# Feed-forward of a trunk layer: sums made ahead take the buffers of gated tiles and GpSimd's queue, and a pass's first operands come in front of the residual

## The chip, the cores and the metric

The kernel runs on one core of a Trainium2 chip. Its time is the device time of one execution, in microseconds (us). The engines of a core work side by side, each through its own list of instructions in order: TensorE (PE; its weight loads are PEld) does matrix products into eight PSUM banks, VectorE (DVE), ScalarE (ACT) and GpSimd (POOL) do elementwise work, and SyncE (SP) does nothing here but issue DMAs. ScalarE and GpSimd issue DMAs too, in the same list as their other work (ACTq and POOLq). An instruction that waits holds up everything behind it on its engine.

## The reference

One layer (DEPTH = 1) on 2048 tokens of width 1024, all float32: a spatial-gating mixer and a cross attention into 256 memory tokens, projected and added to the input, a layer norm, then the part that matters here:

```python
def swiglu_ffn(x, w_in, w_down):
    h = x @ w_in
    return (jax.nn.silu(h[..., :D_FF]) * h[..., D_FF:]) @ w_down

x = layer_norm(DEEPNORM_ALPHA * x + swiglu_ffn(x, ffn_w_in[i], ffn_w_down[i]), ln2_g[i], ln2_b[i])
```

`w_in` is 1024 x 5632, `w_down` 2816 x 1024, so the hidden width is 22 tiles of 128 rows.

## The kernel before

**Exactness.** A float32 product is made of three fast ones. `split` (L71) writes the rounded value (ScalarE's cast, L73) and the remainder (VectorE's subtraction, L74), and `PASSES` multiplies high by high, high by low and low by high. Data lies feature-major, with tokens along the free dimension.

**Seven products.** Matrices are cut in 2 x 2 blocks and multiplied with seven block products in place of eight (a Strassen-Winograd scheme). That needs sums of blocks on both sides. `halves` (L120 on) loads two row tiles of weights (`r_u`, loads at L125) and makes four sums, s1 to s4 (L132, L133, L135, L136), on GpSimd for tiles f < 5 and on VectorE for f >= 5. `products` (L145 on) walks the seven in an order, splits each operand, and runs 12 matmuls on it; after each product a "stage" empties PSUM (L391 to L402).

**Passes and blocks.** The tokens go through the FFN in three passes of 688, 680 and 680. A pass goes through the 22 hidden tiles in blocks (5, 4, 4, 4, 5 tiles in pass 0; 4, 4, 4, 4, 6 in the others). For each tile `up` (L384) makes the two halves of the hidden layer and gates them; after a block `down` or `down7` adds the block's share to the output. In pass 0 `whole` (L418) puts a gated tile, split, into pool "g", and `down` (L558) makes ordinary products. In passes 1 and 2 all blocks but the last go through `down7` (L503), seven products for each pair of output row tiles, with `left` (L456) bringing the operands of one pair: five loads, of which two read `w_down` itself (L479) and three read sums that were made and split before (L90, L464, L471).

**Sums made ahead.** What pass 0 splits for the up products it also stores in DRAM (`keep`, L81, on ScalarE's queue, `k_u`), and passes 1 and 2 read it back (`ready`). For `down7` the sums are made during pass 0: at each of the tiles f = 5 to 20 `left_sums` (L482) makes those of one block and pair, sixteen in all. It is a generator that is moved on once at each of the seven stages of an up tile: load (L485, through `tiles4`), four sums on GpSimd (L491), then two steps that split and store. A leftover of an earlier layer norm (`norm_work`) is moved on in the same way.

**Buffers.** A tile belongs to a pool with so many buffers, and an instruction that writes a new tile waits until all users of the buffer's former tile are done, stores included. "raw" has 4 (`r_u` two a tile, `r_es` and `r_ses` of `left_sums`, `r_d` and `r_e` of the down stages), "wsp" 5 (every split operand; an up tile uses seven, `left_sums` two), "g" 7 (gated tiles; in passes 1 and 2 the seven operands `gp` of `down7`), "sums" 4, "acc" 4 (the residual and result `fa` of a pass, one for each pair of row tiles).

**Order.** TensorE's order is that of the program (`in_order`). The other lists are laid out when the kernel is built, by a planner that goes by what is ready in its own estimate of time and prefers what comes earlier in the program. So the sums of a next tile may stand between the stages of this one.

**The start of a pass.** In passes 1 and 2 the main loop (L998 on) makes the up tiles of block 0 and one of the next block, exhausts `norm_work`, and calls `residual` (L551: four loads from `x1d` into "acc", each of which needs the stores of the pass before, L590, to be done with that buffer). Then `down7` begins with its first `left`.

Of the kernel before, what the change touches and what calls it, by code (L numbers as in the profile page):

```python
# [17 lines left out]
P = 128  # L18
# [21 lines left out]
def trunk_kernel(ctx, tc, xT, memT, wv, wuq, ws, bs, vg, vb, wmk, wmv, wo,  # L40
# [27 lines left out]
    def raw(shape, name):  # L68
        return common.tile(shape, F32, tag="raw", bufs=4, name=name)

    def split(hi, lo, src, engine=nc.vector):  # L71

        nc.scalar.copy(hi, src)  # L73
        engine.tensor_sub(lo, src, hi.bitcast(F32))  # L74

    def wsp(shape, name):
        return common.tile(shape, F32R, tag="wsp", bufs=5, name=name)
# [267 lines left out]
    class Pass:  # L345
# [110 lines left out]
        def left(self, blk, m, f0, q):  # L456

            name, key = f"e{self.no}_{blk}_{m}", f"e{blk}_{m}"
            v = self.tiles4(m, f0, q, name)
            t = ready(f"{key}_5", f"56_{name}")  # L460
            out = {5: t[:, 0], 6: t[:, 1]}
            t = wsp([P, 2, 2, q, P], f"w17_{name}")
            out[1], out[7] = t[:, 0], t[:, 1]
            nc.sync.dma_start(out=t[:, 1].bitcast(F32), in_=kept[f"{key}_7"])  # L464
            split(t[:, 0, 0], t[:, 0, 1], v[:, 0, 0])
            t = wsp([P, 2, 2, q, P], f"w24_{name}")
            out[2], out[4] = t[:, 0], t[:, 1]
            for x in range(2):
                split(t[:, x, 0], t[:, x, 1], v[:, x, 1])
            r = raw([P, 2, q, P], f"w3_{name}")  # L470
            nc.sync.dma_start(out=r, in_=kept[f"{key}_3"])  # L471
            out[3] = r.bitcast(F32R)
            return out

        def tiles4(self, m, f0, q, name):

            r = raw([P, 2, 2 * q, P], f"r_{name}")
            for a in range(2):
                nc.sync.dma_start(out=r[:, a], in_=w2[m + a, :, f0:f0 + 2 * q, :])  # L479
            return r.rearrange("p a (i j) x -> p a j i x", j=2)  # L480

        def left_sums(self, blk, m, f0, q):  # L482

            name, key = f"es{blk}_{m}", f"e{blk}_{m}"
            v = self.tiles4(m, f0, q, name)  # L485
            s = raw([P, 4, q, P], f"r_s{name}")
            yield
            a11, a12, a21, a22 = (v[:, a, j] for a in range(2) for j in range(2))
            for n, (x, y, op) in enumerate(((a21, a22, ALU.add), (s[:, 0], a11, ALU.subtract),
                                            (a11, a21, ALU.subtract), (a12, s[:, 1], ALU.subtract))):  # L490
                nc.gpsimd.tensor_tensor(out=s[:, n], in0=x, in1=y, op=op)  # L491
                yield
            for n, pa in enumerate((5, 7)):
                t = wsp([P, 2, 2, q, P], f"w{pa}_{name}")
                split(t[:, :, 0], t[:, :, 1], s[:, 2 * n:2 * n + 2])
                if n == 0:
                    keep(f"{key}_5", t)
                else:
                    keep(f"{key}_7", t[:, 0])
                    keep(f"{key}_3", t[:, 1])  # L500
                yield

        def down7(self, blk, q, f0, last):  # L503

            h, n, gp = self.h, self.n, self.gp
            if blk == 0:
                self.u = [open_pools["sums"].tile([P, 4, P], F32, tag="sums", name=f"fu{self.no}_{m}")
                          .rearrange("p a b -> p (a b)")[:, 0:h] for m in range(0, KD, 2)]
            w = [self.left(blk, 0, f0, q)]
            banks = []  # L510

            def product(j, p):
                y, u = self.out[j], self.u[j]
                c11, c12, c21, c22 = (y[:, a, b * h:(b + 1) * h] for a in range(2) for b in range(2))
                n, start, stop = {1: (0, True, False), 6: (1, True, True), 2: (0, False, True), 5: (2, True, False),
                                  7: (3, True, False), 3: (2, False, True), 4: (3, False, True)}[p]
                bk = banks[j][n]
                for i in range(q):
                    for x, (a, b) in enumerate(PASSES):
                        matmul(bk, w[j][p][:, a, i, :], gp[p][:, i, b], start=start and i == 0 and x == 0,  # L520
                               stop=stop and i == q - 1 and x == 2, skip_group_check=True)
                if p == 6 and blk == 0:
                    nc.scalar.copy(u, bk)
                    return
                to = {1: u, 6: u, 2: c11, 5: c22, 7: c22, 3: c12, 4: c21}[p]
                if blk == 0 and p in (2, 5, 3, 4):
                    nc.vector.scalar_tensor_tensor(out=to, in0=to, scalar=ALPHA, in1=bk, op0=ALU.mult, op1=ALU.add)
                else:
                    nc.vector.tensor_add(to, to, bk)  # L529

            def second(j):
                for p in (2, 3, 4):
                    product(j, p)
                if last:
                    y, u = self.out[j], self.u[j]
                    nc.vector.tensor_add(y[:, 0, h:n], y[:, 0, h:n], u)
                    nc.vector.tensor_tensor(out=y[:, 1].rearrange("p (b t) -> p b t", b=2),
                                            in0=y[:, 1].rearrange("p (b t) -> p b t", b=2),
                                            in1=u.unsqueeze(1).broadcast_to([P, 2, h]), op=ALU.add)

            for j in range(KD // 2):
                if j < KD // 2 - 1:
                    w.append(self.left(blk, 2 * j + 2, f0, q))
                banks.append([bank(f"e{i}_{self.no}_{blk}_{j}")[:, 0:h] for i in range(4)])
                for p in (6, 1, 5, 7):
                    product(j, p)
                if j:
                    second(j - 1)
            second(KD // 2 - 1)
# [427 lines left out]
    for no in range(len(FPASSES)):  # L977
# [20 lines left out]
        for blk, nb in enumerate(blocks):  # L998
            end = blk == len(blocks) - 1
            fs = range(f0 + len(ahead), f0 + nb)  # L1000
            if no and not end:
                ys = list(ahead)
                for f in fs:
                    ys.append(up(f))
                    if len(ys) % 2 == 0:
                        side.append((pa.pair(len(ys) // 2 - 1, blk, ys[-2][1], ys[-1][1]), 2))
                ahead = [up(f0 + nb)]
            else:
                gs = [pa.whole(*y) for y in ahead] + [pa.whole(*up(f)) for f in fs]
                ahead = []  # L1010
            if blk == 0:
                for _ in norm_work:
                    pass
                pa.residual()
            if no and not end:
                pa.down7(blk, nb // 2, f0, blk == len(blocks) - 2)
            elif not end:
                pa.down(blk, gs, f0, whole, lambda ci, m: None)
            elif no < len(FPASSES) - 1:
# [92 lines left out]
```

## Time and profile before

| | |
|---|---|
| median of 3 runs | 2264.46 us (2261.26 to 2265.94) |
| the profiled execution | 2261.46 us, its span 2259.6 us |
| TensorE busy | 2118.9 us, 94% of the span |
| VectorE, ScalarE, GpSimd busy | 71%, 40%, 17% |
| mean granted TensorE clock | 0.979 of full speed |
| moved by DMA | 408 MB, 181 GB/s |
| up stages of pass 0, blocks 1 to 4 | 878.6 to 949.5, 979.6 to 1050.6, 1082.4 to 1153.0, 1184.7 to 1282.3 us |
| first `down7` of pass 1, of pass 2 | from 1396.0 us, from 1852.2 us |

How to read the profile: a line of groups gives the source line, engine, operation, "written <- read" with shapes, the count, the busy time, the mean of one in ns, and after the second bar the idle time of the engine just before them, with what ended it. Names come from the tiles: `h` are PSUM banks of an up tile, `d` of `down`, `e` of `down7`; `s_u`, `r_u`, `w` belong to the up products, `r_es`, `r_ses`, `w_es`, `k_e` to the sums made ahead, `w_e` to the operands that `left` brings. A line in order of time starts with its start and its duration and joins like neighbours. "SPq" is SyncE's DMA queue.

### The profile page before, as it was taken

Reading aid. Unit: us, or ns where it says so; the run is one execution under the profiler, and the core shown is the slowest. Engines: PE = TensorE matmul, PEld = TensorE weight load, DVE = VectorE, ACT = ScalarE, POOL = GpSimd, SP = SyncE. Lnnn points to the kernel's source line nnn. Section 1 sums busy time; section 2 is a strip of 40 time slices with the busy share of each in tenths; the row PEclk is TensorE's granted clock in tenths of the full one; section 3 lists DMA queues with packets and bytes.
Section 4 is the critical chain, followed back from the end, with each engine's and each line's share of the span. In section 5 each row is a group of like instructions: output and inputs, shape, how many; then the busy total and the mean of one; then the engine's idle time right before and its main releaser. Section 6 shows DMA issues by size and latency. Waiting matters only on the chain.

```text
span 2259.6 us, 35072 instructions
## 1 busy us (share of the span) xinstructions
PE 2118.9 (94%) x12938; PEld 1995.0 (88%) x12938; DVE 1614.5 (71%) x2966; ACT 908.3 (40%) x1814; POOL 389.7 (17%) x318
## 2 busy tenths in 40 slices
PE   9899999999999889898898898999999989999997
PEld 7888888798788789788888788999999979999996
DVE  7987896796798876666667676566666765666656
ACT  5553743653554443333324344223323342233234
POOL 1402322321331611111111140000000400000002
PEclk9999999999999999999999899999999999999998
DMA  6234233425235474645556557666665576666653
GB/s 206 75 115 138 93 109 116 133 67 162 97 98 164 171 249 171 231 182 205 207 193 224 178 198 259 224 239 217 233 231 176 174 260 237 227 226 231 227 181 99
DMA packets 152331, 408.12 MB, mean 181 GB/s; under 512 B 15456, under 2 KB 25696, under 8 KB 152160
## 3 DMA queue, kind: packets, MB, share of 16 engines
q1 hardware_dynamic: 132096, 341.89, 45.3%
q10 hardware_dynamic: 19584, 62.92, 7.2%
q8 instruction: 102, 1.67, 0.3%
q0 software_dynamic: 480, 1.07, 0.2%
q14 instruction: 69, 0.57, 0.1%
HBM read 326.13 MB, written 79.69 MB: 180 GB/s over the span
## 4 chain that ended last, share of the span: by engine, by line
PE 61%; DVE 18%; DMA 9%; issue 5%; ACT 4%; POOL 2%; ACTq 0%; SPq 0%; DVEq 0%; POOLq 0%
PE h L60 30%; PE e L60 9%; PE d L60 9%; PE v L60 5%; DMA r_u<-in_w 3%; PE u L60 3%; DVE w L74 2%; DMA r_x<-in_xT 2%; PE y L60 2%; DVE w_o L74 1%; DVE w_u L74 1%; DVE x L74 1%; POOL s_a L233 1%; ACT p L740 1%; DVE z L697 1%
## 5 line engine op out<-in xcount | busy, mean ns | idle before, releaser
L60 PE MATMUL h<-x,w 128*128 128x340 f32 (+1 forms) x5544 | 910.1, 325 | 67.4 <-DVE w L74 20.7
L60 PEld LDWEIGHTS h<-x,w 128*128 128x128 f32 x5544 | 886.1, 192 | 87.0 <-DVE w L74 29.4
L60 PE MATMUL d<-g,w_d 128*128 128x344 f32 (+3 forms) x1632 | 266.9, 324 | 12.2 <-ACT w_d L73 6.6
L60 PEld LDWEIGHTS d<-g,w_d 128*128 128x128 f32 x1632 | 260.5, 191 | 17.1 <-ACT w_d L73 7.4
L60 PE MATMUL e<-gp,w_e 128*128 128x340 f32 x1344 | 214.4, 321 | 14.7 <-DMA w_e<-k_e 14.7
L60 PEld LDWEIGHTS e<-gp,w_e 128*128 128x128 f32 x1344 | 212.6, 190 | 15.4 <-DMA w_e<-k_e 15.2
L60 PE MATMUL y<-br,w_o 128*128 128x512 f32 x960 | 224.2, 395 | 0.0
L60 PEld LDWEIGHTS y<-br,w_o 128*128 128x128 f32 x960 | 180.5, 188 | 41.8
L73 ACT CAST w<-r_u 128x512 fp32r<-128x512 f32 x198 | 122.0, 617 | 183.6 <-PE h L60 117.5
L60 PE MATMUL v<-w_v,x 128*128 128x512 f32 x768 | 188.2, 401 | 6.4 <-ACT w_v L73 4.8
L74 DVE TENSOR_TENSOR w<-r_u,w 128x512 fp32r<-128x512 f32 x198 | 150.0, 758 | 49.8 <-ACT w L73 42.3
L60 PEld LDWEIGHTS v<-w_v,x 128*128 128x128 f32 x768 | 143.6, 190 | 42.2 <-ACT w_v L73 4.8
L60 PE MATMUL u<-xt,w_u 128*128 128x256 f32 x768 | 95.6, 279 | 0.0
L369 POOL TENSOR_TENSOR t<-r_f,r_f 128x340 f32<-128x340 f32 (+1 forms) x12 | 13.9, 1156 | 461.9 <-DVE c L392 376.7
L60 PEld LDWEIGHTS u<-xt,w_u 128*128 128x128 f32 x768 | 92.7, 188 | 0.0
L529 DVE TENSOR_TENSOR fa<-fa,e 128x340 f32<-128x340 f32 x128 | 64.6, 506 | 38.1 <-PE e L60 36.0
L491 POOL TENSOR_TENSOR r_ses<-r_es 128x256 f32<-128x256 f32 x32 | 28.8, 920 | 362.7 <-DMA r_es<-in_w 181.5
L60 PE MATMUL u<-x,w_u 128*128 128x256 f32 x576 | 77.8, 286 | 11.9 <-DVE u L706 7.1
L73 ACT CAST w_d<-r_d 128x384 fp32r<-128x384 f32 (+2 forms) x104 | 52.7, 519 | 88.8 <-PE d L60 65.6
L74 DVE TENSOR_TENSOR w_o<-r_o,w_o 128x512 fp32r<-128x512 f32 (+1 forms) x96 | 69.0, 728 | 21.4 <-ACT w_o L73 21.3
L60 PEld LDWEIGHTS u<-x,w_u 128*128 128x128 f32 x576 | 71.4, 189 | 14.6 <-issue 7.0
L393 ACT ACTIVATE c<-c 128x340 f32<-128x340 f32 (+1 forms) x66 | 32.3, 489 | 128.6 <-DVE c L392 128.6
(206 smaller groups left out, 2894.5 us busy)
## 6 DMA issues: line engine op xcount, KB each, us to landing
w<-k_u SPq DMA_DIRECT2D x176, 512.0 KB, 4.3
r_u<-in_w SPq DMA_DIRECT2D x88, 512.0 KB, 3.6
k_u<-w ACTq DMA_DIRECT2D x88, 512.0 KB, 3.4
r_u<-in_wuq SPq DMA_DIRECT2D x32, 512.0 KB, 3.2
r_o<-in_wo SPq DMA_DIRECT2D x32, 512.0 KB, 3.5
r_e<-in_w SPq DMA_DIRECT2D x64, 256.0 KB, 2.9
w_e<-k_e SPq DMA_DIRECT2D x64, 256.0 KB, 3.2
w_e<-k_e SPq DMA_DIRECT2D x32, 512.0 KB, 4.0
```

Of the source, the lines that this page charges most:

```text
L60: in_order(nc.tensor.matmul(*args, **kw))
L73: nc.scalar.copy(hi, src)
L74: engine.tensor_sub(lo, src, hi.bitcast(F32))
L233: nc.gpsimd.tensor_add(self.s2, self.s2, sq)
L369: nc.gpsimd.tensor_sub(t3, b22, b12)
L393: nc.scalar.activation(c12, c12, AF.Silu)
L491: nc.gpsimd.tensor_tensor(out=s[:, n], in0=x, in1=y, op=op)
L529: nc.vector.tensor_add(to, to, bk)
L697: nc.vector.tensor_scalar(z[h][:, b], z[h][:, b], mv[:, b, 0:1], rs[:, b:b + 1], ALU.subtract, ALU.mult)
L740: nc.scalar.activation(pr[:, h, :], svs[h // 2][:, h % 2, :], AF.Exp, scale=HD ** -0.5, bias=mxv[:, h:h + 1], accum_out=sm[:, h:h + 1])
```

## The change

Two things are changed.

1. `left_sums` takes both its tiles, r and s, from pool "g" (they have a fixed shape of 4 x q x 128 a partition, 4 KB, under a gated tile's 5.5 KB). Its two loads are issued on GpSimd's queue (`tiles4` with a tile given). It no longer takes "wsp" tiles: when the four sums are done, the high halves are written over r and the low halves over s, in place. The stores stay on ScalarE's queue; there are four of 256 KB (high and low of each pair of sums) in place of one of 512 KB and two of 256 KB, into DRAM tiles that interleave high and low, so that what was the tile `_3` is now the second half of `_7`. `left` reads the same data as before, out of that half.
2. In passes 1 and 2 the first `left` of a block is called by the main loop and handed to `down7`. For block 0 that is ahead of `residual`; for the other blocks the order of the program is the same as before.

```diff
@@ -461,52 +461,51 @@
-            nc.sync.dma_start(out=t[:, 1].bitcast(F32), in_=kept[f"{key}_7"])
+            nc.sync.dma_start(out=t[:, 1].bitcast(F32), in_=kept[f"{key}_7"][:, 0])
...
             r = raw([P, 2, q, P], f"w3_{name}")
-            nc.sync.dma_start(out=r, in_=kept[f"{key}_3"])
+            nc.sync.dma_start(out=r, in_=kept[f"{key}_7"][:, 1])
             out[3] = r.bitcast(F32R)
             return out
 
-        def tiles4(self, m, f0, q, name):
-
-            r = raw([P, 2, 2 * q, P], f"r_{name}")
+        def tiles4(self, m, f0, q, name, r=None):
+
+            queue = nc.sync if r is None else nc.gpsimd
+            r = raw([P, 2, 2 * q, P], f"r_{name}") if r is None else r
             for a in range(2):
-                nc.sync.dma_start(out=r[:, a], in_=w2[m + a, :, f0:f0 + 2 * q, :])
+                queue.dma_start(out=r[:, a], in_=w2[m + a, :, f0:f0 + 2 * q, :])
             return r.rearrange("p a (i j) x -> p a j i x", j=2)
 
         def left_sums(self, blk, m, f0, q):
 
             name, key = f"es{blk}_{m}", f"e{blk}_{m}"
-            v = self.tiles4(m, f0, q, name)
-            s = raw([P, 4, q, P], f"r_s{name}")
+            r, s = (open_pools["g"].tile([P, 4, q, P], F32, tag="g", name=f"{x}_{name}") for x in "rs")
+            v = self.tiles4(m, f0, q, name, r.rearrange("p (a i) j x -> p a (i j) x", a=2))
             yield
             a11, a12, a21, a22 = (v[:, a, j] for a in range(2) for j in range(2))
             for n, (x, y, op) in enumerate(((a21, a22, ALU.add), (s[:, 0], a11, ALU.subtract),
                                             (a11, a21, ALU.subtract), (a12, s[:, 1], ALU.subtract))):
                 nc.gpsimd.tensor_tensor(out=s[:, n], in0=x, in1=y, op=op)
                 yield
+            hi, lo = r.bitcast(F32R), s.bitcast(F32R)
             for n, pa in enumerate((5, 7)):
-                t = wsp([P, 2, 2, q, P], f"w{pa}_{name}")
-                split(t[:, :, 0], t[:, :, 1], s[:, 2 * n:2 * n + 2])
-                if n == 0:
-                    keep(f"{key}_5", t)
-                else:
-                    keep(f"{key}_7", t[:, 0])
-                    keep(f"{key}_3", t[:, 1])
+                k = slice(2 * n, 2 * n + 2)
+                split(hi[:, k], lo[:, k], s[:, k])
+                t = kept[f"{key}_{pa}"] = dram.tile([P, 2, 2, q, P], F32, tag=f"{key}_{pa}", name=f"k_{key}_{pa}")
+                for x, part in enumerate((r, s)):
+                    nc.scalar.dma_start(out=t[:, :, x], in_=part[:, k])
                 yield
 
-        def down7(self, blk, q, f0, last):
+        def down7(self, blk, q, f0, last, w):
...
-            w = [self.left(blk, 0, f0, q)]
             banks = []
@@ -1008,12 +1007,15 @@
+            seven = no and not end
+            if seven:
+                first = [pa.left(blk, 0, f0, nb // 2)]
             if blk == 0:
                 for _ in norm_work:
                     pass
                 pa.residual()
-            if no and not end:
-                pa.down7(blk, nb // 2, f0, blk == len(blocks) - 2)
+            if seven:
+                pa.down7(blk, nb // 2, f0, blk == len(blocks) - 2, first)
```

## The prediction

> **What bounds the kernel now.** I began with the stretches of the span by engine, one row per stage. In pass 0 the up stages of blocks 1 to 4 (tiles f = 5 to 21, the ones with sums made ahead up to f = 20) are rows 1, 2, 3 and 4; the fifth row is a part of pass 1.
>
> ```profile
> core 0: us, PE busy (x) PEld busy (x) DVE busy (x) ACT busy (x) POOL busy (x), PEclk, DMA share, GB/s
> 878.60:949.50 70.90, 59.02 (x340) 55.75 (x338) 50.90 (x83) 28.14 (x55) 11.79 (x12) 0.95 0.67 237
> 979.60:1050.60 71.00, 58.66 (x339) 55.64 (x337) 48.38 (x81) 28.37 (x55) 11.75 (x12) 0.95 0.64 229
> 1082.40:1153.00 70.60, 58.57 (x338) 55.28 (x336) 49.10 (x81) 28.30 (x55) 11.82 (x12) 0.95 0.66 230
> 1184.70:1282.30 97.60, 79.48 (x434) 75.26 (x432) 62.29 (x106) 36.52 (x72) 12.71 (x13) 0.88 0.60 209
> 1430.00:1666.00 236.00, 236.00 (x1515) 236.00 (x1514) 153.15 (x312) 69.12 (x151) 0.00 (x0) 1.00 0.66 228
> ```
>
> In pass 1 TensorE never stops. In pass 0 it does, and its granted clock falls to 0.95 and 0.88. The chain of waits says what 84 matmuls of an up tile should cost: in the first row 72 of them run without a gap, 11.38 / 72 × 84 = 13.3 us a tile. Seventeen tiles would be 226 us; the four stretches together are 70.9 + 71.0 + 70.6 + 97.6 = 310.1. So 84 us are lost here, the largest loss in the FFN.
>
> ```profile
> 979.63 11.38 PE h L60 x72
> 1399.95 5.88 DMA w_e<-k_e
> ```
>
> Next the instructions in order of time of one such stage (the second row): first TensorE's, then SyncE's DMA queue, then one line of VectorE and one of ScalarE. In brackets stands the idle time before, and what ended it.
>
> ```profile
> 979.47 22.85 PE L60 MATMUL h<-x,w 128*128 128x344 f32 x144
> 1005.40 5.58 PE L60 MATMUL h<-x,w 128*128 128x344 f32 x24 [3.08 <-DVE c L401]
> 1013.16 9.67 PE L60 MATMUL h<-x,w 128*128 128x344 f32 x50 [2.19 <-ACT w L73]
> 1024.74 1.84 PE L60 MATMUL h<-x,w 128*128 128x344 f32 x10 [1.90 <-DVE w L74]
> 1030.40 14.01 PE L60 MATMUL h<-x,w 128*128 128x344 f32 x84 [0.90 <-DVE w L74]
> 1045.90 1.84 PE L60 MATMUL h<-x,w 128*128 128x344 f32 x10 [1.50 <-DVE w L74]
> 1049.93 2.53 PE L60 MATMUL d<-g,w_d 128*128 128x344 f32 x7 [2.19 <-ACT w_d L73]
> ```
> ```profile
> 988.39 0.80 SPq L479 DMA_DIRECT2D r_es<-in_w  x2
> 995.70 1.30 SPq L125 DMA_DIRECT2D r_u<-in_w  x2
> 1018.16 0.84 SPq L125 DMA_DIRECT2D r_u<-in_w  x2
> ```
> ```profile
> 1004.14 0.69 DVE L132 TENSOR_TENSOR s_u<-r_u 128x512 f32<-128x512 f32 x1 [5.26 <-DMA r_u<-in_w]
> 1004.40 0.62 ACT L73 CAST w_es<-r_ses 128x512 fp32r<-128x512 f32 x1 [3.31 <-DMA k_u<-w]
> ```
>
> The story is in these lines. The pool "raw" has four buffers. An up tile needs two (r_u); the sums made ahead need two more (r_es and r_ses). So the next tile's r_u is issued alternately with r_es and only when those are given back: at 995.70, while the first of its sums stands in VectorE's order already. VectorE waits 5.26 us for the landing, and behind it stand the additions that empty PSUM (L401) and the low halves of the weights (L74): TensorE stops 3.08, then 2.19, then 1.90 us. ScalarE has a stop of its own there: the cast for the ahead sums waits 3.31 us for a "wsp" buffer that a store still reads. The totals, from the groups by line and from the queue's waits (the latter count the mixer too):
>
> ```profile
> L132 DVE TENSOR_TENSOR s_u<-r_u 128x512 f32<-128x512 f32 x17 | 11.7, 691 | 41.7 <-DMA r_u<-in_w 41.7
> L491 POOL TENSOR_TENSOR r_ses<-r_es 128x256 f32<-128x256 f32 x32 | 28.8, 920 | 362.7 <-DMA r_es<-in_w 181.5 <-DVE w_d L74 130.4 <-DVE w L74 35.9
> SPq L125 <- POOL r_ses L491: 54.1, 13, 5.1
> SPq L125 <- DMA r_es<-in_w: 37.1, 17, 3.3
> ```
>
> **Part 1: the ahead sums leave "raw" and "wsp".** Both r and s of L482 to L501 now come from pool "g", and the halves are written in place over them. "raw" then holds r_u of two tiles, and r_u of tile f+1 can be issued once tile f-1 has given its two buffers back, about a tile time (13 us) before it is wanted, against the 8.4 us from issue at 995.70 to use at 1004.14. So VectorE's 41.7 us of waits should go. What is late next? VectorE's own work. Rows 1 to 3 hold 48.4 to 50.9 us of it in four tiles, under the 53.2 us that TensorE needs for four, so it still fits, though at 91 to 96%, and some of it can move into the down stages in between, where it is idle for 13 of 32 us:
>
> ```profile
> 1050.60:1082.40 31.80, 31.75 (x192) 31.75 (x193) 18.54 (x32) 5.80 (x10) 2.85 (x4) 0.95 0.44 151
> ```
>
> I don't expect the whole 84 us. Three prices for a tile after the change: 13.3 us (all loss gone: 226 us for seventeen, a gain of 84); the 84 matmuls at 1030.40 with the gap before them, 14.01 + 0.90 = 14.9 us, a stretch where no load is late; and 16.4 us, from 1024.74 to 1047.74 (1045.90 + 1.84), where 118 matmuls take 23.0 us with VectorE still catching up. I take the middle one, since the catching up is caused by the late load: 17 × 14.9 = 253, and the 2.19 us ahead of the down stage, which the late load doesn't make, stays three times: 6.6. So 260 in place of 310: **50 us** less. With 16.4 it is 279 + 6.6, a gain of 25. The bounds of this part are 25 and 84, and there is a loss only by the rival below.
>
> Pool "g" must have room. It has seven buffers; at the k-th tile of a block k-1 hold gated tiles and two the sums before, which leaves 6-k, two at k = 4. Only the first tile of blocks 2 to 4 finds one free, and there 30 us of a down stage lie between. I cost it at nothing; without that cover it is one store's landing, 4.0 us, three times:
>
> ```profile
> k_e<-w_es ACTq DMA_DIRECT2D x16, 512.0 KB, 3.1
> k_e<-w_es ACTq DMA_DIRECT2D x32, 256.0 KB, 4.0
> r_es<-in_w SPq DMA_DIRECT2D x32, 256.0 KB, 3.0
> wm<-in_ws POOLq DMA_DIRECT2D x1, 512.0 KB, 6.5
> 5.03 0.53 POOL L603 DMA_DIRECT2D wm<-in_ws  x1
> 1013.96 2.21 POOL L491 TENSOR_TENSOR r_ses<-r_es 128x256 f32<-128x256 f32 x2 [18.28 <-DVE w L74]
> 1014.35 1.23 DVE L74 TENSOR_TENSOR w<-r_u,w 128x512 fp32r<-128x512 f32 x1
> ```
>
> **Part 2: the two loads move from SP's queue to GpSimd's.** Thirty-two issues leave SP, and GpSimd gets 32 × 0.53 us, 1.06 us a tile, on an engine that is busy 11.8 of 71 us. A load on that queue landed after 6.5 us (512 KB, at the start of the kernel) against 3.0 us on SP's. Behind the waiting issue on GpSimd stand only the four additions of L491 (0.92 us each and the like), and for those waits the cast in ScalarE's order. The loads are free of "raw" and can run a tile ahead, so I cost this at 0; uncovered it is 6.5 - 3.0 + 1.06 = 4.6 us a tile, 73 us for sixteen.
>
> The Trainium skill, SBUF — State Buffer, section "SBUF: two separate sides", speaks against this move: descriptors of a DMA issued from GpSimd are written by its cores, which are locked out while VectorE holds the shared ports, and it advises ScalarE's or SyncE's queue instead. The same page, section "A bandwidth-pool intuition that's wrong (but worth ruling out)", gives 620 ns alone and 3100 ns overlapped for one such DMA; as an estimate from that page, 2.5 us × 32 loads would be 79 us if nothing hid them. Contention of the two engines shows in this trace (the VectorE operation at 1014.35 took 1.23 us beside GpSimd's additions, the one at 1004.14 without them 0.69); a GpSimd-issued load beside VectorE's work, none here shows.
>
> **Part 3: the stores.** Four of 256 KB a tile on ScalarE's queue in place of one of 512 and two of 256: the same bytes, one issue more, in runs of half the length in DRAM. Nearest row: 4.0 us to landing. Nothing of the up products waits for these any more. ScalarE is busy 28 of 71 us, so 0; not below nothing, because no store goes; at most an issue of about 0.8 us on the path, 16 × 0.8 = 13. Reading `_7` and `_3` out of one DRAM tile keeps 256 KB a load: 0.
>
> **Part 4: a pass's first operands ahead of the residual.** SyncE's queue, TensorE and ScalarE at the start of the down stage of pass 1, block 0:
>
> ```profile
> 1393.10 0.37 SPq L554 DMA_DIRECT2D fa<-x1d  x1
> 1394.07 5.83 SPq L554 DMA_DIRECT2D fa<-x1d  x3
> 1399.95 0.63 SPq L464 DMA_DIRECT2D w_e<-k_e  x1
> 1401.17 0.36 SPq L464 DMA_DIRECT2D w_e<-k_e  x1
> ```
> ```profile
> 1389.09 0.39 ACT L73 CAST w_e<-r_e 128x256 fp32r<-128x256 f32 x1
> 1396.00 2.96 PE L60 MATMUL e<-gp,w_e 128*128 128x340 f32 x18
> 1405.88 19.37 PE L60 MATMUL e<-gp,w_e 128*128 128x340 f32 x114 [6.91 <-DMA w_e<-k_e]
> 1862.92 17.40 PE L60 MATMUL e<-gp,w_e 128*128 128x340 f32 x100 [7.78 <-DMA w_e<-k_e]
> ```
>
> Three products (18 matmuls) run, and the fourth waits 6.91 us for L464, which stood behind four residual loads. ScalarE's cast at 1389.09 writes the other half of the same tile, so its buffer was free before the first residual at 1393.10. Ahead of the residual the load is there in time. But the second group's L464 (1401.17) stays behind: its product 7 is wanted 42 matmuls after 1396.00, 42 × 2.96 / 18 = 6.9 us, at 1402.9, and its load, issued at about 1400 with the same 5.9 us, lands at 1406. So some 3.1 us stay, and 3.8 and 4.7 are won: I take 3 a pass, **6 us** in all, because the residual now lands a little later too and the addition L527 needs it. Bounds: 0, if the second group's wait takes all of it, and 14.7.
>
> **Sum.** 50 + 6 = 56 us off the profiled execution's own 2261.46 (span 2259.6), 2205.5; the median of the runs shown stands 3.0 us above that execution, so I predict **2208**.
>
> **Rivals.**
> 1. VectorE becomes the bound. For it: 91 to 96% of the time of the matmuls, and 1.23 us operations beside GpSimd. Against: the first tiles of each stage already run without a gap. Tiles at 16.4 us: gain 25, with part 4 about 31: 2233.
> 2. All the loss goes, the clock back to 1.00 as in pass 1: 84 + 14.7 = 99: 2166. Against: the fourth tile still has 1.50 and 2.19 us of gaps of other makers.
> 3. Slower: GpSimd's loads come late, at the cast of the ahead sums (L495). ScalarE takes its list in order, so behind that cast wait the high halves of the next weights and L393, and for them TensorE. Price 4.6 us a tile, 73 in all, less the 56 won: 17 more, 2281. It decides from 56 / 16 = 3.5 us of stop a tile. For it: 6.5 us against 3.0. Against: "g" has a free pair of buffers at nearly every tile, so that the load has a tile's time. The SBUF page of the Trainium skill, quoted in part 2, is for this rival.
> 4. It does nothing: r_u stays late, because r_d of the down stages takes the free "raw" buffers or the order of SP's queue doesn't move. Against: SP waited for r_es and r_ses by name. About 2262.
>
> **Chances.** Forecast (gain 40 to 70 us) 0.53; rival 1 0.22; rival 2 0.10; rival 3 0.08; rival 4 0.07. Forecast and rivals 1 and 2 are all faster by more than 0.2% (4.5 us, about what can be told from no change here): faster 0.85, same 0.07, slower 0.08. The range leaves out most of rivals 3 and 4 and the far end of 2: from 2264 - 86 = 2178 to 2250, above rival 1 by its unpriced stores of 13 us and some.
>
> **What would show it.** VectorE's group L132 without its 41.7 us of DMA waits; r_u issues of SP a tile ahead; the up stages of blocks 1 to 3 at 58 to 64 us and the last at 72 to 80, granted clock near 1.00; the wait on w_e of the fourth product gone and one of about 3 us three products later. Wrong: TensorE or ScalarE waiting for GpSimd's r_ses, up stages still near 71 us, or a wait of the first addition L527 for the residual.

## The result, and the profile after

The changed kernel takes 2200.40 us (median; 2199.23 to 2201.72), the kernel before on the same chip 2264.69 us: a ratio of 0.972, 95% interval 0.970 to 0.974. The prediction was 2208. The profiled execution of the changed kernel has a span of 2197.5 us against 2259.6, 62.1 us less.

Read first the stretches by engine (as in the prediction: the busy time of each engine in a stretch, then the granted clock). Rows 1 to 3 are the up stages of pass 0, blocks 1 to 3; row 4 is that of block 4 with 1.8 us of the down stage behind it; row 5 is the down stage of block 2.

```profile
core 0: us, PE busy (x) PEld busy (x) DVE busy (x) ACT busy (x) POOL busy (x), PEclk, DMA share, GB/s
876.60:934.20 57.60, 54.19 (x338) 52.73 (x336) 44.91 (x78) 25.37 (x50) 13.30 (x16) 1.00 0.73 259
965.50:1023.00 57.50, 54.09 (x337) 52.62 (x337) 43.53 (x75) 25.39 (x50) 10.43 (x13) 1.00 0.72 249
1054.30:1112.00 57.70, 54.29 (x337) 52.82 (x336) 43.72 (x76) 25.39 (x50) 10.34 (x13) 1.00 0.71 249
1143.40:1217.00 73.60, 69.42 (x432) 67.69 (x432) 57.02 (x101) 33.77 (x68) 9.27 (x11) 1.00 0.71 247
1023.00:1054.30 31.30, 30.54 (x194) 30.26 (x195) 23.23 (x39) 8.05 (x15) 9.66 (x12) 1.00 0.62 215
```

The stages of four tiles fell from about 71 to 57.6 us, and the granted clock in them is 1.00 where it was 0.95 and 0.88. VectorE has 43.5 to 44.9 us of work in them (before: 48.4 to 50.9), and the down stage between them took some of it over, 23.23 us where it had 18.54.

For comparisons I take a stage exactly, from its first matmul to the first of the next stage. The four up stages are then 305.8 us before (70.3 + 70.5 + 70.1 + 94.9; the prediction's stretches, 310.1, took in the starts of down stages) and 244.7 after (57.5 + 57.6 + 57.7 + 72.0): **61.0 us of the 62.1 lie there.**

TensorE's instructions in order of time, in the second of these stages and the first two of the down stage; in brackets the idle time before and what ended it:

```profile
965.31 40.26 PE L60 MATMUL h<-x,w 128*128 128x344 f32 x252
1006.00 0.58 PE L60 MATMUL h<-x,w 128*128 128x344 f32 x2 [0.43 <-ACT w L73]
1007.81 11.60 PE L60 MATMUL h<-x,w 128*128 128x344 f32 x72 [1.23 <-DVE w L74]
1020.31 1.85 PE L60 MATMUL h<-x,w 128*128 128x344 f32 x10 [0.90 <-DVE w L74]
1022.87 0.58 PE L60 MATMUL d<-g,w_d 128*128 128x344 f32 x2 [0.72 <-ACT w_d L73]
1024.21 30.05 PE L60 MATMUL d<-g,w_d 128*128 128x344 f32 x190 [0.76 <-DVE w_d L74]
```

Three tiles, 252 matmuls, run without a stop at 40.26 / 3 = 13.4 us each. Only the last tile of a stage still has gaps, of about a microsecond each. The groups of instructions by line, and below them two of VectorE's first additions in order of time:

```profile
L60 PE MATMUL h<-x,w 128*128 128x344 f32 x1848 | 302.9, 324 | 22.4 <-DVE w L74 9.6 <-ACT w L73 4.6 <-ACT m L400 4.3
L132 DVE TENSOR_TENSOR s_u<-r_u 128x512 f32<-128x512 f32 x17 | 12.6, 741 | 14.5 <-DMA r_u<-in_w 14.3
```
```profile
948.73 0.69 DVE L132 TENSOR_TENSOR s_u<-r_u 128x512 f32<-128x512 f32 x1 [3.52 <-DMA r_u<-in_w]
996.79 0.68 DVE L132 TENSOR_TENSOR s_u<-r_u 128x512 f32<-128x512 f32 x1
```

VectorE's wait for raw weights fell from 41.7 to 14.3 us. Of what is left, 12.2 us stand in places like 948.73, inside a down stage, where no up product is waiting behind it; the rest are waits of 0.6 to 0.9 us early in an up stage, where TensorE has no stop. The addition at 996.79, in the up stage, found its weights there. Where before one such addition stood 5.26 us, TensorE now runs on.

The other part, the start of a pass, from SyncE's queue and then from TensorE:

```profile
1326.43 0.43 SPq L464 DMA_DIRECT2D w_e<-k_e  x1
1327.90 4.07 SPq L553 DMA_DIRECT2D fa<-x1d  x4
1332.02 0.70 SPq L90 DMA_DIRECT2D w_e<-k_e  x1
```
```profile
1330.32 3.91 PE L60 MATMUL e<-gp,w_e 128*128 128x340 f32 x24
1341.88 25.34 PE L60 MATMUL e<-gp,w_e 128*128 128x340 f32 x144 [7.65 <-DMA w_e<-k_e]
```

The load L464 of the first group now stands ahead of the residual (L553), and all four products of that group (24 matmuls) run. The fifth waits 7.65 us. Before, the fourth waited 6.91. From the first matmul of this stage to the next up stage it is 36.7 us (34.7 before), in pass 2 35.0 (35.8 before): together 71.7 against 70.5. Nothing was won here in these two executions.

### The profile page after: what moved, and what is told of

Its sections match the earlier page's. It is cut to its first block, busy times and chain, and to the rows that moved or that the text cites. A ratio compares the mean times of both kernels' runs of the same rounds, so it can differ in the third digit from the quotient of the medians.

```text
span 2197.5 us, 35099 instructions
## 1 busy us (share of the span) xinstructions
PE 2096.4 (95%) x12938; PEld 1979.8 (90%) x12938; DVE 1608.6 (73%) x2966; ACT 905.6 (41%) x1814; POOL 411.5 (19%) x350
## 4 chain that ended last, share of the span: by engine, by line
PE 65%; DVE 17%; DMA 7%; ACT 4%; issue 4%; POOL 2%; ACTq 0%; SPq 0%; DVEq 0%; POOLq 0%
PE h L60 34%; PE e L60 9%; PE d L60 8%; PE v L60 5%; PE u L60 3%; PE y L60 3%; DMA r_f<-x1d 2%; DMA r_x<-in_xT 1%; DVE w L74 1%; DVE x L74 1%; DVE w_o L74 1%; DVE w_u L74 1%; POOL s_a L233 1%; ACT p L739 1%; DMA w_e<-k_e 1%
## 5 line engine op out<-in xcount | busy, mean ns | idle before, releaser
L60 PE MATMUL h<-x,w 128*128 128x340 f32 (+1 forms) x5544 | 887.8, 321 | 32.0 <-DVE w L74 11.4
L60 PEld LDWEIGHTS h<-x,w 128*128 128x128 f32 x5544 | 870.4, 189 | 44.9 <-DVE w L74 16.6
L60 PE MATMUL e<-gp,w_e 128*128 128x340 f32 x1344 | 216.0, 322 | 14.3 <-DMA w_e<-k_e 14.3
L369 POOL TENSOR_TENSOR t<-r_f,r_f 128x340 f32<-128x340 f32 (+1 forms) x12 | 13.5, 1127 | 464.4 <-DMA r_f<-x1d 461.3
L60 PEld LDWEIGHTS u<-x,w_u 128*128 128x128 f32 x576 | 71.3, 189 | 13.6 <-issue 6.5
L74 DVE TENSOR_TENSOR w_d<-r_d,w_d 128x384 fp32r<-128x384 f32 (+2 forms) x104 | 67.6, 662 | 21.0 <-ACT w_d L73 20.6
L73 ACT CAST gp<-c 128x340 fp32r<-128x340 f32 x112 | 51.8, 476 | 74.6 <-DVE c L398 42.0
```

The costliest lines, as they stand in the source:

```text
L60: in_order(nc.tensor.matmul(*args, **kw))
L369: nc.gpsimd.tensor_sub(t3, b22, b12)
```

## The experiments

The table gives for each kernel the time, the ratio to the kernel before (executed beside it on the same chip) with its interval, the four up stages of pass 0 measured as above, and the first down stages of passes 1 and 2 added up. A stage of that last kind without any wait takes 26.2 us (block 1 of either pass), so two of them 52.4.

| kernel | median us | ratio, 95% | up stages | first down stages |
|---|---|---|---|---|
| before | 2264.69 | | 305.8 | 70.5 |
| after | 2200.40 | 0.972, 0.970 to 0.974 | 244.7 | 71.7 |
| a1_g_only | 2227.32 | 0.984, 0.982 to 0.986 | 266.7 | 70.7 |
| a2_in_place_only | 2252.32 | 0.995, 0.993 to 0.997 | 292.2 | 72.0 |
| a3_queue_only | 2266.58 | 1.001, 1.000 to 1.002 | 309.2 | 68.8 |
| a4_after_sp | 2216.41 | 0.979, 0.978 to 0.981 | 258.3 | 70.3 |
| a5_first_left_only | 2262.93 | 0.9988, 0.9979 to 0.9997 | 309.6 | 71.8 |
| a6_no_first_left | 2205.94 | 0.9733, 0.9720 to 0.9746 | 247.0 | 70.9 |
| b1_residual_pool | 2202.80 | 0.9725, 0.9712 to 0.9737 | 244.8 | 59.3 |
| b2_two_lefts | 2206.08 | 0.9740, 0.9727 to 0.9752 | 249.6 | 68.9 |
| b3_residual_pool_later | 2196.08 | 0.9698, 0.9678 to 0.9718 | 244.7 | 60.8 |
| c1_low_on_pool | 2207.80 | 0.975, 0.974 to 0.977 | 247.7 | 70.6 |
| d1_s_in_raw | 2234.99 | 0.987, 0.984 to 0.989 | 274.7 | 71.0 |
| e1_loads_on_act | 2224.87 | 0.983, 0.982 to 0.985 | 262.1 | 72.5 |

The stages are of one execution each, and block 0 of pass 0, which comes ahead of all of them, begins at 750 to 756 us and takes 126 to 130 us (133 in b1) in these profiles. So a difference of a few us between medians proves little unless the stages show it too. Nor are the stages exact: a5 changes nothing in pass 0, and its up stages come out 3.8 us longer than before.

### Parts one at a time

**Only the pool.** The kernel before, with r and s of `left_sums` in "g"; SP's queue, the splits into "wsp" and the three stores stay.

```diff
-            v = self.tiles4(m, f0, q, name)
-            s = raw([P, 4, q, P], f"r_s{name}")
+            r, s = (open_pools["g"].tile([P, 4, q, P], F32, tag="g", name=f"{x}_{name}") for x in "rs")
+            v = self.tiles4(m, f0, q, name, r.rearrange("p (a i) j x -> p a (i j) x", a=2))
```

> The kernel before, with r and s of the sums made ahead in pool "g" and nothing else: loads on SyncE's queue, splits into "wsp", three stores, the residual first. Theory T (the four "raw" buffers make r_u late): r_u has all of "raw", so 45 to 62 us of the 64 are won, VectorE's wait for r_u under 10 us in the up stages of pass 0. Rival W (the "wsp" buffers that stores hold stop ScalarE): under 15 us won. Rival Q (r_es, waiting at the head of SyncE's queue, holds r_u behind it): as T here, since r_es finds its buffer free; the run with the queue alone tells these two apart.

Measured: 0.984, up stages 305.8 to 266.7. By the medians 35.6 us are won (2262.92 to 2227.32 on that chip), fewer than the 45 to 62 of the first theory and far more than the rival's 15. The groups say that the late weights are gone (row 1), and TensorE's and ScalarE's waits between 860 and 1260 us say what is late next (rows 2 to 4: waited for, us in total, times, longest):

```profile
L132 DVE TENSOR_TENSOR s_u<-r_u 128x512 f32<-128x512 f32 x17 | 11.7, 687 | 2.1 <-DMA r_u<-in_w 1.8
...
PE h L60 <- ACT w L73: 11.8, 5, 2.5
...
PE d L60 <- ACT w_d L73: 6.6, 3, 2.2
...
ACT g L73 <- DVE w_es L74: 8.7, 4, 2.2
```

TensorE's waits of the kernel before, between 860 and 1290 us, to hold against them:

```profile
PE h L60 <- DVE c L401: 16.0, 5, 5.9
PE h L60 <- ACT w L73: 12.9, 9, 2.2
```

The stops behind VectorE's additions (L401), 16.0 us before, have gone but for 1.0; those behind ScalarE's casts have stayed, 11.8 and 6.6 us (the row with 6.6 is the same before). ScalarE's list still holds the ahead sums' own splits, and casts of gated tiles there wait for their low halves (`w_es`). So 39.1 of the 61.0 us are the pool alone, and the rest needs the other edits.

**Only in place.** r and s in "raw", halves written over them, four stores.

```diff
-                t = wsp([P, 2, 2, q, P], f"w{pa}_{name}")
-                split(t[:, :, 0], t[:, :, 1], s[:, 2 * n:2 * n + 2])
+                k = slice(2 * n, 2 * n + 2)
+                split(hi[:, k], lo[:, k], s[:, k])
```

> The kernel before, with the halves of the sums made ahead written over r and s in "raw" (no "wsp" tiles, four stores), loads still on SyncE's queue. Theory T: "raw" is as short as before, or shorter, because r and s now stay until the stores have landed (3 to 4 us more): 0 to 20 us slower. Rival W: 40 us or more faster, ScalarE's 12.3 us of waits for stores gone.

Measured: 0.995, up stages 292.2, 13.5 us less; VectorE still waits 36.4 us for `r_u` (by the same group of additions). So the halves in place, with their four stores, are worth something, though the late weights stay; neither expectation (0 to 20 us slower, or 40 faster) came true. Here too TensorE's stops behind L401 are nearly gone, 0.9 us, while 19.3 us of stops stand behind low halves (17.8 before) and 7.9 behind ScalarE's copies (L400): a stop changes its name from kernel to kernel, and only the length of the stage says what was won.

**Only the queue.** The kernel before, with the two loads issued by GpSimd.

```diff
-                nc.sync.dma_start(out=r[:, a], in_=w2[m + a, :, f0:f0 + 2 * q, :])
+                queue.dma_start(out=r[:, a], in_=w2[m + a, :, f0:f0 + 2 * q, :])   # nc.gpsimd from left_sums
```

> The kernel before, with only the two loads of the sums made ahead issued from GpSimd's queue in place of SyncE's; buffers as before. Theory T: r_u still waits for "raw": within 10 us of the kernel before, on either side. Rival Q: r_u no longer stands behind r_es in the queue, 45 us or more faster.

Measured: 1.001, no difference. The buffers of "raw" still go round. SP's largest wait is now that of the `r_u` loads for a buffer that the ahead sums hold; by this name it was 37.1 us before (us in total, times, longest):

```profile
SPq L125 <- DMA r_es<-in_w: 188.1, 13, 18.5
```

### The queue, with the pool

**The changed kernel with its loads back on SP's queue.**

```diff
-            queue = nc.sync if r is None else nc.gpsimd
+            queue = nc.sync
```

> The changed kernel with the two loads of the sums made ahead back on SyncE's queue. Theory T: the queue is worth nothing, so within 5 us of the changed kernel (2195 to 2206). Rival Q: 45 us or more of the gain lost. Rival of the Trainium skill (loads issued from GpSimd starve beside VectorE's work): 5 to 15 us faster than the changed kernel, landing 3.0 us in place of 4.6.

Measured: 0.979; 16 us of the gain are gone, of which 13.5 in the up stages. The same edit that was worth nothing by itself is worth a quarter of the whole when the tiles are in "g". SP's queue (rows 1 and 2), then ScalarE and TensorE, in order of time:

```profile
960.37 26.22 SPq L125 DMA_DIRECT2D r_u<-in_w  x4
986.70 0.85 SPq L480 DMA_DIRECT2D r_es<-in_w  x2
```
```profile
996.54 1.14 ACT L73 CAST r_es<-s_es 128x512 fp32r<-128x512 f32 x2 [3.41 <-POOL s_es L492]
999.07 2.71 PE L60 MATMUL h<-x,w 128*128 128x344 f32 x14 [0.76 <-DVE c L402]
```

`r_u` may now be asked for a tile ahead, so its issues stand at the head of SP's list and wait there for a "raw" buffer: four of them take 26.22 us to go. Behind them stands `r_es`, which needs no "raw" buffer at all; it goes at 986.70. The sums come late, the cast waits 3.41 us for them, and TensorE stops for 0.76 us. Against the first matmul of the stage (973.60) the load is 13.1 us behind. In the changed kernel it goes at 964.84, 0.5 us ahead of that matmul, when the pair of "g" buffers is free. The stage takes 61.2 us here and 57.6 there. This is a block in the order of one list. It is no matter of the landing, which takes as long from either queue, by the DMA issues of the changed kernel and of this one (KB each, us from issue to landing):

```profile
r_es<-in_w POOLq DMA_DIRECT2D x32, 256.0 KB, 4.6
r_es<-in_w SPq DMA_DIRECT2D x32, 256.0 KB, 4.7
```

(With the old buffers it was 3.0 us from SP's queue, the row in the prediction, and 3.7 from GpSimd's, in a3.)

**ScalarE's queue in place of GpSimd's.**

```diff
-            queue = nc.sync if r is None else nc.gpsimd
+            queue = nc.sync if r is None else nc.scalar
```

> The changed kernel with the two loads of each ahead sum issued by ScalarE in place of GpSimd. Theory (what the move to GpSimd's queue was worth, some 16 us against the same kernel with these loads on SP's, comes from leaving the list in which the loads of raw weights wait for their buffers, so any other list does): near the changed kernel, if ScalarE finds its pair of gated-tile buffers free when it gets to the issue, 2198 to 2206 us. Where it has to wait there for the last sum's store to land, casts stand behind it: up to 3.5 us for each of 16 loads, and the time lies between 2206 and 2256 us, with ScalarE's issue of the load waiting by name for a store of ahead sums. Rival (the worth of GpSimd's queue comes from something else, a queue of its own for the descriptors or a later start of the loads): as with SP's queue, 2213 to 2220 us, and TensorE's gaps behind VectorE's additions as there.

Measured: 2224.87, 0.983; up stages 262.1, worse than on SP's queue. The time is in the range that the theory left for stops at the issue, but not by that mechanism: no wait of ScalarE for a store of ahead sums is among its waits. It simply gets to the issue late. GpSimd's list in the changed kernel, ScalarE's here, and the stop that follows:

```profile
964.84 1.09 POOL L480 DMA_DIRECT2D r_es<-in_w  x2 [9.47 <-PE d L60]
```
```profile
988.71 0.34 ACTq L480 DMA_DIRECT2D r_es<-in_w  x1
996.89 1.15 ACT L73 CAST r_es<-s_es 128x512 fp32r<-128x512 f32 x2 [3.94 <-POOL s_es L492]
1002.40 12.31 PE L60 MATMUL h<-x,w 128*128 128x344 f32 x74 [2.38 <-ACT w L73]
```

On ScalarE's list the load stands behind the casts and copies of the tile before, and these wait for TensorE: it goes 15.3 us behind the stage's first matmul (973.41). So "any list but SP's" is wrong: of the three lists tried, only the one with nothing else waiting at its head is worth 13.5 us. GpSimd's is that here: it works 10 of 57 us. The Trainium skill, SBUF — State Buffer, section "SBUF: two separate sides", by which this load belongs on ScalarE's or SyncE's queue, would have cost 16 to 24 us here. A load that lands late from GpSimd's queue because VectorE is at work does not show between the changed kernel and a4 (4.6 and 4.7 us); with the old buffers there are 0.7 us of difference (3.7 and 3.0). The Trainium skill, DMA: Bandwidth & Descriptors, section "Issuing engines are not separate DMA queues", says that another issuing engine saves only the time of the issues. Those take 0.85 us a tile on SP (986.70), 13.6 us for sixteen, which is the size of this gain by chance only: the run with the queue alone takes the same issues off SP and wins nothing.

### How the buffers count

**One of the two tiles back in "raw".**

```diff
-            r, s = (open_pools["g"].tile([P, 4, q, P], F32, tag="g", name=f"{x}_{name}") for x in "rs")
+            r = open_pools["g"].tile([P, 4, q, P], F32, tag="g", name=f"r_{name}")
+            s = raw([P, 4, q, P], f"s_{name}")
```

> The changed kernel with one of the two tiles of each ahead sum, the one that holds the sums and then the low halves, back in a buffer of the raw weights; the loaded tile stays with the gated tiles. Before the change both had stood there. Theory (the time that an ahead sum holds a raw buffer is what kept the raw weights from running ahead, and each of the two tiles counts with the time it is held): held from the first sum to the landing of the last store, one tile costs about half of the 47 to 60 us that came from this part, 2222 to 2230 us, with the wait of VectorE's sums for raw weights back between 14.5 and 41.7 us. Rival (only the loaded tile counted, since it is asked for on the list of SP, ahead of the raw weights' loads): within 5 us of the changed kernel, 2198 to 2206 us. Rival (what counts is that any one is taken from the four): as before the change but for the stores and the queue, 2245 us or more.

Measured: 2234.99, up stages 274.7: 30.0 of the 61.0 us are lost, about half, as the first theory has it (the time came out 5 us above its range, and VectorE's wait for raw weights at 19.1 us, inside it). The loss is uneven, 13.9, 6.1, 5.8 and 4.1 us in the four stages, so the half is only their sum. "Only the loaded tile" falls, and "any one of the four", for which 2245 us or more were expected, by 10 us. SP's list names the holder: the loads of raw weights wait until the store of s has landed (rows 1 and 2), a wait that the changed kernel doesn't have by that name.

```profile
SPq L125 <- DMA k_e<-s_es: 94.7, 13, 14.3
...
SPq L104 <- DMA k_e<-s_es: 73.0, 7, 19.1
```

**Is VectorE the bound now?** The low halves of the ahead sums subtracted on GpSimd.

```diff
-                split(hi[:, k], lo[:, k], s[:, k])
+                split(hi[:, k], lo[:, k], s[:, k], nc.gpsimd)
```

> The changed kernel with the low halves of the ahead sums subtracted on GpSimd instead of VectorE: 32 operations of 128x512 leave VectorE and come to GpSimd behind the sums. Theory (after the change TensorE sets the pace of pass 0's up stages and VectorE has some 13 of 57 us free in each): the gaps that TensorE has behind VectorE's splits of w there are about 10 us in the whole kernel, of which a part goes; GpSimd has about 45 us of 57 free; 2190 to 2201 us. Rival (VectorE is the bound of these stages, as the first rival of the prediction had it): the stages fall with VectorE's load by some 8 operations of 1.2 us each, 10 us a stage, 2160 us or so. If GpSimd's operations and VectorE's slow one another, the time rises, 2205 us or more.

Measured: 2207.8, slower than the changed kernel and in the range given for operations of the two engines that slow one another. The second stage by engine:

```profile
970.52:1027.93 57.41, 54.41 (x339) 52.68 (x337) 41.22 (x68) 25.46 (x50) 18.67 (x19) 1.00 0.70 240
```

VectorE has 2.3 us less to do than in the changed kernel, GpSimd 8.2 us more, and the stage takes 57.4 against 57.6 us. So VectorE's load doesn't set the length of these stages, and the first rival falls for them. The loss lies elsewhere: the last up stage (75.4 against 72.0), the down stages (about 0.7 us each), and 4.5 us ahead of the first up stage, 3.1 of them ahead of the FFN's first matmul, where the edit changes nothing. VectorE's low halves of the sums' weights did get slower, by the groups of after and then of this kernel, 773 to 900 ns:

```profile
L74 DVE TENSOR_TENSOR w<-s_u,w 128x512 fp32r<-128x512 f32 x88 | 66.7, 773 | 10.3 <-ACT w L73 9.5
```
```profile
L74 DVE TENSOR_TENSOR w<-s_u,w 128x512 fp32r<-128x512 f32 x88 | 77.9, 900 | 11.5 <-ACT w L73 10.1
```

That this made the last stage longer isn't shown.

### The start of a pass

**Part 4 alone, and the changed kernel without it.**

```diff
+            seven = no and not end
+            if seven:
+                first = [pa.left(blk, 0, f0, nb // 2)]
             if blk == 0:
                 ...
                 pa.residual()
```

> The kernel before with part 4 alone: the first operands of down7 ahead of the residual in passes 1 and 2. The prediction's step: 6 us faster (0 to 14.7). What the changed kernel's trace suggests: the wait moves from the fourth product to the fifth, on the second group's operands, which now stand behind the residual: between 2 us faster and 3 us slower.

> The changed kernel without part 4: the residual first again. If part 4 is worth nothing, 2198 to 2204, as the changed kernel; if the prediction's 6 us are in it, 2204 to 2209.

Measured: 0.9988 alone; without it 0.9733 against 0.9719 with it, intervals that overlap. Both pairs of medians speak for some 3 us, and a6's 2205.94 lies in the range that was named for the prediction's 6. But in the place that the edit touches there is nothing: the two first down stages add up to 70.5 us before and 71.8 with part 4 alone, 71.7 after and 70.9 without it, in one execution each. So the few us between the medians aren't shown to be its work; the interval of a5 leaves room for under 5.

**Two groups' operands ahead of the residual.**

```diff
-                first = [pa.left(blk, 0, f0, nb // 2)]
+                first = [pa.left(blk, m, f0, nb // 2) for m in ((0, 2) if blk == 0 else (0,))]
```

> The changed kernel with the operands of two groups ahead of the residual in place of one, all on SyncE's queue. If the order in the queue makes the wait: the 14.3 us go but the residual lands later, and 3 to 12 us are won (2188 to 2197); VectorE's L527 or its like then waits for the residual. If bandwidth makes it: within 4 us of the changed kernel.

`down7` then takes as many groups as it is given before it asks for more. Measured: 0.9740, not faster than the changed kernel and in neither of the expected ranges; its up stages, which the edit doesn't touch, are 4.9 us longer. The first down stages add up to 68.9 us. TensorE's order in pass 1:

```profile
1342.92 8.58 PE L60 MATMUL e<-gp,w_e 128*128 128x340 f32 x54
1351.81 2.14 PE L60 MATMUL e<-gp,w_e 128*128 128x340 f32 x12 [0.31 <-DVE fa L526]
1359.26 17.85 PE L60 MATMUL e<-gp,w_e 128*128 128x340 f32 x102 [5.31 <-DMA w_e<-k_e]
```

The stop moves on from the 24th to the 66th matmul and is still 5.31 us, and now the addition L526 waits for the residual as well. Whatever comes behind the four residual loads on this list is late.

**The residual on GpSimd's queue,** in all passes (b1), then in passes 1 and 2 alone (b3).

```diff
-                nc.sync.dma_start(out=y, in_=two_tiles(x1d, m, self.t0, self.n))
+                nc.gpsimd.dma_start(out=y, in_=two_tiles(x1d, m, self.t0, self.n))                          # b1
+                (nc.gpsimd if self.no else nc.sync).dma_start(out=y, in_=two_tiles(x1d, m, self.t0, self.n))  # b3
```

> The changed kernel with the residual loads on GpSimd's queue, so that nothing stands behind them. If the second group's operands are late because they stand behind the residual in SyncE's queue: the waits on w_e (14.3 us) go, and 6 to 14 us are won on the changed kernel (2186 to 2194). If they are late because 2.7 MB of residual take the DMA engines: the waits stay within 4 us, and the time within 4 us of the changed kernel's.

> The changed kernel with the residual's four loads on GpSimd's queue in passes 1 and 2 alone; in pass 0 they stay on SP's. Theory (in the down stages of pass 1 and 2 the residual's four transfers take the place of the second group's load; in pass 0, where GpSimd has the ahead sums to do, moving them costs the 9 us that the run with all residual loads moved lost there): the start of the seven-product stage of passes 1 and 2 falls from 36.7 and 35.0 us to about 31.0 and 28.4, pass 0 stays as after the change, 2187 to 2193 us. Rival (the 9 us lost in pass 0 with all of them moved were no loss of pass 0 but the same wait at another place, or what pass 1 and 2 gain comes back as a later load): 2199 to 2203 us.

Measured: b1 2202.80, no different from the changed kernel; b3 2196.08. In both the first down stages fall from 71.7 to about 60 us. TensorE in b3, pass 1:

```profile
1334.81 6.70 PE L60 MATMUL e<-gp,w_e 128*128 128x340 f32 x42
1342.98 4.03 PE L60 MATMUL e<-gp,w_e 128*128 128x340 f32 x24 [1.48 <-DMA w_e<-k_e]
1349.03 16.16 PE L60 MATMUL e<-gp,w_e 128*128 128x340 f32 x102 [2.02 <-DMA w_e<-k_e]
```

7.65 us have become 3.5, and in the whole kernel the waits on `w_e` fell from 14.3 to 7.1 us. So the order of the list was about half of them, and each of the two explanations that b1 set against one another is half right. The rest isn't the order: the load that ends the last of these waits has no residual load ahead of it on its list, and lands late all the same, while the residual's transfers are under way (6.3 to 10.7 us each):

```profile
1338.75 10.14 DMA w_e<-k_e
```

From the first matmul of this stage to the end of the span b3 takes 2190.8 - 1334.8 = 856.0 us, the changed kernel 867.2: 11.2 us won. But b3 reached the stage 4.5 us later, in a part of the program that the edit doesn't change, so that the median shows 4 us; the intervals of b3 and of the changed kernel overlap, and I call b3 the best of the kernels run, not a proved one. Its expected 2187 to 2193 was missed by 3 us, less than that late start. In b1 the residual of pass 0 stood in GpSimd's list ahead of the first load of ahead sums:

```profile
827.79 2.17 POOL L553 DMA_DIRECT2D fa<-x1d  x3 [3.85 <-issue]
829.96 1.11 POOL L480 DMA_DIRECT2D r_es<-in_w  x2
844.35 1.40 POOL L492 TENSOR_TENSOR s_es<-r_es 128x256 f32<-128x256 f32 x2 [13.28 <-DMA r_es<-in_w]
```

The load went at 829.96, 77.3 us after the first matmul of the FFN (752.7); in the changed kernel it is 68.5 (818.90, from 750.4). And block 0 of pass 0 took 133.2 us, against 126.0 after and 128.8 in b3. So some 4 to 7 us of b1's gain were lost there; how much of it is that list, and how much the variation of block 0, isn't settled.

## Why the prediction was right, and where not

**The bound and part 1 were right.** The stages that the prediction named gave 61.0 of the 62.1 us, by the step that it named: buffers of "raw" held by the ahead sums kept `r_u` back (one of the two tiles put back there, half of the gain lost). Part 1 has not all of the 61.0. With the loads left on SP's queue (a4) the four stages take 258.3 us, where the prediction's sum for them was 260: 47.5 us won, against the forecast of 50, which counted from 310.1 and so from 4.3 us too many. The other 13.5 are part 2. With both, a tile takes 244.7 / 17 = 14.4 us, and three of four run at 13.4. One term of the sum was wrong: the 2.19 us ahead of a down stage were to stay, three times, and fell to 0.72. These waits are 6.6 us in all with the pool alone, 0.8 with the halves in place alone, 2.1 in a4 and 2.2 after; but they are 6.6 in d1 too, which makes the halves in place, so what sets them isn't shown.

**Part 2 was costed at nothing: wrong.** Its step was "The loads are free of "raw" and can run a tile ahead", which is true only on a list where nothing waits ahead of them. Part 1 is what makes SP's list wait: 13.5 us of the up stages, 16 us of the median. The prediction looked at what the move costs GpSimd and the landing (4.6 us, hidden, as it said), and not at what would stand ahead of these loads on SP once part 1 was done. That the forecast of the whole still came so near is luck in part: these 13.5 us, put at nothing, stood in for the 6 of part 4 that did not show, and what they have above these 6 is about what the gain has above the forecast of 56.

**Part 3, put at nothing, was not tested by itself:** the stores' edit was only run together with the in-place halves, a gain each time (13.5 us alone, 8.4 on top of the pool, 258.3 against 266.7, though that kernel has part 4 too). The prediction counted those halves into part 1.

**Part 4: forecast 6, measured none in its place.** The step that failed is "what is late next". The prediction took it to be the second group's L464, wanted 42 matmuls after the start. But that group's other load, from L90, is wanted after 24, and it too stands behind the residual: issued at 1332.02, it ends the chain's wait at 1341.84.

```profile
1332.02 9.82 DMA w_e<-k_e
```

It took 9.82 us to land, against the 5.88 that the prediction took over: four residual loads issued back to back just ahead of it were on their way too, 6.5 to 9.4 us each. Six matmuls more of cover, 1 us, met a load as late as the one before. In these stages the value was the lower bound of 0; by the medians it may be a few us above.

**Rivals.** VectorE as the bound falls (c1). All the loss gone: no, 61 of about 80 us, though the clock is back at 1.00 there as that rival had it. GpSimd's loads late: no, moving them there won 13.5 us. Nothing: falls. Of the signs named, the up stages came in just below the forecast's 58 to 64, and the last at the lower end of 72 to 80; the wait on `w_e` did not shrink to 3 us three products later, it moved one product on and stayed at 7.65.

## What to carry to other kernels

When a buffer pool is relieved, the loads that run ahead will wait at the head of their queue: look at what stands behind them there, and move those that need another pool to a list with nothing else waiting, whichever engine it belongs to. Price edits together, not one by one: pool, in-place halves and queue gave 39, 13.5 and 0 us of the up stages alone (against 61 together). Before a transfer is moved ahead of a bulk of others, list every load that then stands behind the bulk with the moment it is wanted; if one is wanted a microsecond later, move the bulk to another queue instead, which took off about half of the wait here.

## What was not expected of the hardware

ScalarE's issue of a store into the interleaved DRAM tile takes 0.52 us where one of the contiguous stores takes 0.33, in order of time:

```profile
909.12 0.33 ACTq L83 DMA_DIRECT2D k_u<-w  x1
912.72 0.53 ACTq L500 DMA_DIRECT2D k_e<-r_es  x1
```

And a part of the gain came by TensorE's granted clock. Two down stages of the kernel before, those of blocks 1 and 2, have the same 192 matmuls and hardly a stop; at a clock of 0.95 in place of 1.00 the second takes 1.56 us longer (by engine, as in the result):

```profile
948.76:979.47 30.71, 30.57 (x193) 30.28 (x193) 19.04 (x33) 6.48 (x11) 3.20 (x4) 1.00 0.50 166
1049.93:1082.20 32.27, 32.12 (x192) 31.84 (x193) 19.21 (x33) 6.47 (x11) 2.85 (x4) 0.95 0.46 157
```

The four up stages had 0.95 three times and 0.87 before and have 1.00 now. As an estimate, what these clocks lack times the length of their stages is some 23 us. The group of all up matmuls of pass 0 agrees: its busy time fell by 22.6 us (325.5 to 302.9) and its idle time by 36.0 (58.4 to 22.4), so about a third of the gain may be the clock's.

```profile
L60 PE MATMUL h<-x,w 128*128 128x344 f32 x1848 | 325.5, 337 | 58.4 <-DVE w L74 18.9 <-DVE c L401 18.8 <-ACT w L73 15.4
```

The low clocks went with the stops: 2 to 3 us in these stages before, 0.3 to 1.4 after. No size of stop marks the border, though: the second stage of e1 has one of 2.38 us at 1.00, that of a4 none above 1.39 at 0.97. That the stops bring the clock down isn't shown, since no run here changes one without the other.
